# Weight sums in DRAM made in quarters of 512 KB with their copies on SP's queue, and retention's first operands loaded earlier

## The chip, the cores and the metric

The kernel runs on one core of a Trainium2 chip. The metric is the device time of one execution in microseconds (us). The core's engines are TensorE (PE in the profile, its weight loads PEld), VectorE (DVE), ScalarE (ACT), GpSimd (POOL) and SyncE (SP). Each runs its own instructions in order; semaphores tie them together. DMAs are issued by SP (queue q1 in the profile) and by GpSimd (queue q0).

## The reference, cut to what matters

One decoder block on x (1024 tokens, 1024 channels, float32). A normalised and modulated h goes through one wide projection, whose parts feed retention (4 heads, keys of 256, values of 512, in chunks of 128 tokens) and three groups of dilated attention:

```python
proj = h @ w_in
rq = rotary(heads(rq, 4), pos); rk = rotary(heads(rk, 4), pos) * 256 ** -0.5
ro = retention(rq, rk, heads(rv, 4))
ret_out = (silu(rg) * group_norm(ro)) @ w_ret_out
att_out = att @ w_att_out
merged = sigmoid(gate_a) * ret_out + sigmoid(gate_b) * att_out
x = x + g1 * (merged @ w_o)
x = x + g2 * (square(relu(h2 @ w1)) @ w2)
```

The change touches how the weights of rv (`w_rv`) and `w_ret_out` are prepared, and when retention's first q, k, v and gate weights are loaded.

## The kernel before

**Arithmetic.** Each float32 operand is split into a high part that TensorE takes as it is and a low rest: ScalarE copies the high part, VectorE subtracts it, and `mm3` (L201, L203, L205) makes three matmuls of 128x512 for one product. Large products are done by a scheme with seven block products in place of eight ("11", "s1", "s3", "s2", "12", "22", "s4" in `ORDER`), for which sums of weight blocks and sums of blocks of h are needed.

**The order of the work** is written out by hand: the program's order is each engine's order. The stages around the change are, in order, `av_first` and `av_step` (values of attention, PE `av`), `queries_keys` (PE `qap`), `values` (retention's values, PE `va`, `vb`, `vc`) and `chunk` (retention, PE `rg`, `kv`, `o`).

**Queries, keys and gates.** `queries_keys` runs 18 pairs of output blocks through the class `Blocks` (L243 to L285), seven products of 12 matmuls each, 84 matmuls a pair. For the pair two ahead, `before` issues two weight loads of 512 KB on SP (`a_load`, L874, tile `wa`) when a pair starts. `prep` splits a block of weights as soon as a slot is free (ScalarE L248, VectorE L258, tile `qaw`; sums of blocks on VectorE L243, tile `qas`), `post` evacuates the banks (L280, L284, L285, L903, L905), `rotate` (L927) applies the rotation to a pair of q or k, and results go to DRAM on SP (`aqd`, `gated` L915, `qkd` L930). Preparations and evacuations share ScalarE and VectorE in program order: a preparation that waits for a load or for a buffer holds up the evacuations behind it, and those give PE its banks back.

**The weight sums** are made in DRAM by DMAs that GpSimd issues (`weight_sums`, L541 to L551), called once at the start of `queries_keys`. Each of the two matrices has four blocks of 2 MB. `dma_sum` copies one operand (L535) and adds the other with an accumulating DMA (L536): s1 = b21 + b22, s3 = b21 + b11, s2 = s1 + b11, s4 = s2 + b12. Then three plain copies follow (L551). All are 2 MB, 22 DMAs in all (tiles `wrv..`, `wro..`). A small GpSimd multiply (L543) holds the first until the last sum of h is there.

**Retention's values.** `values` runs 14 products (i = 0 to 13), each in four quarters p of 12 matmuls. Weights of product i + 2 are loaded when product i starts (L984, `vwl`), and split during product i - 1 (`v_w`, `v_low`). Results that are complete are split (L1027 to L1034) into tiles `vo` of the pool `wraw`, or for "s4" into `vr`, and stored (L1036, `vd`). The pool `wraw` has three buffers, which the weight loads of `Steps` use as well.

**Retention's entry.** At the end of `values` come, before the change:

- at i = 12, p = 3: `fetch(0)`, which loads q and k of chunks 0 and 1 (L574, `qk`) and v of chunk 0 (L582);
- at i = 13, p = 0: eight restores of h from DRAM by GpSimd (L1061, L1062, `hh`, `hl`), and `first["release"]`, which lets `Steps` issue its next three loads (L85: gate weights and two rows of modulation weights);
- at i = 13, p = 1: `jit_qk(0)` and `jit_qk(1)`, which split q and k of chunks 0 and 1 (ScalarE L594, GpSimd L595, tile `j`);
- at i = 13, p = 2: `ahead(2)`, which splits the first gate weights (L191, L192) and takes one modulation product (L450).

Then the pool of the stage is closed, `fetch(1)` and `fetch(2)` follow, and `s_kt(0)` makes chunk 0's scores and transposed keys (PE `sT`, `kT`; L617 to L628, the last of them `kl`). The PSUM banks are laid out anew after it, and PE's first matmuls of retention (`rg`) wait for `kl`.

Of the kernel before, what the change touches and what calls it, by code (L numbers as in the profile page):

```python
# [11 lines left out]
F32 = mybir.dt.float32  # L12
F32R = mybir.dt.float32r
AF = mybir.ActivationFunctionType
ALU = mybir.AluOpType
AX = mybir.AxisListType

P = 128
D = 1024
S = 1024  # L20
NK = D // P
# [33 lines left out]
class Steps:  # L55
# [12 lines left out]
    def add(self, body, loads=(), manual=False):  # L68

        self.steps.append((list(loads), body, manual))  # L70
# [64 lines left out]
def block_kernel(ctx, tc, io, stop=None, dbg=None):  # L135
# [3 lines left out]
    def fv(t):  # L139
        return t.bitcast(F32)  # L140
# [385 lines left out]
    YB = ("11", "12", "21", "22")  # L526

    WN = ("11", "12", "22", "s1", "s2", "s3", "s4")
    wv_d = {n: dram.tile([P, 4, 1024], F32, name=f"wrv{n}") for n in WN}
    ws_d = {n: dram.tile([P, 4, 1024], F32, name=f"wro{n}") for n in WN}  # L530

    def dma_sum(out, x, y):

        flat = lambda t: t.rearrange("p a b -> p (a b)").rearrange("p (a b) -> p a b", b=2048)
        nc.gpsimd.dma_start(flat(out), flat(x))  # L535
        nc.gpsimd.dma_start(flat(out), flat(y), accum_op=ALU.add, max_dma_last_dim=8192)  # L536

    def weight_sums(t):

        for i, v in enumerate((VC_GNG, VC_GNB)):  # L540
            nc.vector.tensor_copy(gnv[i][:, :16], vec[:, v:v + 16])  # L541
            nc.vector.tensor_scalar_mul(gnv[i][:, 16:], vec[:, v:v + 16], -1.0)
        nc.gpsimd.tensor_tensor(pad[:, NK:NK + 1], fv(t)[:, :1], mhalf[:, :1], op=ALU.mult)  # L543
        for dst, src in ((wv_d, io["w_rv"]), (ws_d, io["w_ret_out"])):
            b11, b12, b21, b22 = (src[i] for i in range(4))
            dma_sum(dst["s1"], b21, b22)
            dma_sum(dst["s3"], b21, b11)
            dma_sum(dst["s2"], dst["s1"], b11)
            dma_sum(dst["s4"], dst["s2"], b12)
            for n, b in (("11", b11), ("12", b12), ("22", b22)):  # L550
                nc.gpsimd.dma_start(dst[n], b)  # L551

    def result_sums():
        b11, b12, b21, b22 = (y_d[:, i] for i in range(4))
# [10 lines left out]
    def fetch(i):  # L565

        h, c = divmod(i, NC)
        if i > 1:
            hd["qk", i] = R["p"].tile([P, 4, C], F32, tag="qk", bufs=4, name=f"qk{h}{c}")
        elif i == 0:  # L570
            t = whl.tile([P, 1024], F32, tag="wl", name="qk01").rearrange("p (a b c) -> p a b c", a=2, b=4)
            for j in range(2):
                hd["qk", j] = t[:, j]
                nc.sync.dma_start(t[:, j], qk_d[0][:, :, j * C:(j + 1) * C])  # L574
        if i > 1:
            nc.sync.dma_start(hd["qk", i], qk_d[h][:, :, c * C:(c + 1) * C])
        if i > 0:
            v = R["p"].tile([P, 2, DV], F32R, tag="V", bufs=4, name=f"v{h}{c}")
        else:
            v = whl.tile([P, 1024], F32R, tag="wh", name="v00").rearrange("p (a b) -> p a b", a=2)  # L580
        hd["v", i] = v
        nc.sync.dma_start(fv(v), v_d[h][:, c])  # L582
# [4 lines left out]
    def jit_qk(i):  # L587
        src = hd["qk", i]
        if i > 1:
            t = R["p"].tile([P, 2, 4, C], F32R, tag="j", bufs=2, name=f"j{i}")  # L590
        else:
            t = whl.tile([P, 1024], F32R, tag=("wh", "wl")[i], name=f"j{i}")
            t = t.rearrange("p (a b c) -> p a b c", a=2, b=4)
        nc.scalar.copy(t[:, 0], src)  # L594
        nc.gpsimd.tensor_sub(t[:, 1], src, fv(t[:, 0]))  # L595
        hd["j", i] = t
# [337 lines left out]

    def queries_keys(ahead):
        sums_of_h("t4")
        weight_sums(XA["t4", 3][1])
        sums = [(q, n) for q in range(NA) for n in ORDER][4:]
        while len(BA.slots) > 1:
            BA.prep(sums.pop(0))  # L940

        def before(q, n):
            if n == ORDER[0] and q + 2 < NA:
                for part in (1, 2):
                    a_load(q + 2, part)

        turns = []

        def after(q, n):
            if turns:  # L950
                next(turns[0], None) or None
            if n == ORDER[-1] and PAIRS[q][0] == "r":
                while turns:
                    drain(turns.pop())
                turns.append(rotate(q))
            if q == NA - 1 and n in ("12", "s4"):
                v_load(n == "s4")
            if q == NA - 1 and n == "22":
                for j in range(2):
                    v_w(0, j)  # L960

        BA.run([(q, n) for q in range(NA) for n in ORDER], sums, before, after)
        while turns:
            drain(turns.pop())
        values(ahead)


# [11 lines left out]
    def v_load(i):  # L979

        hp, n = VSEQ[i]
        for j in range(2):
            lo = V["w", i, j] = v_place(i, "l", j)
            nc.sync.dma_start(fv(lo), wv_d[n][:, 2 * hp + j])  # L984

    def v_w(i, j):
        lo, hi, sign = V["w", i, j], v_place(i, "h", j), float(VPLAN[VSEQ[i][1]][1])
# [4 lines left out]
    def v_low(i, j):  # L992
        lo, hi, sign = V.pop(("low", i, j))
        if sign > 0:
            nc.vector.tensor_sub(lo, fv(lo), fv(hi))
        else:
            nc.vector.scalar_tensor_tensor(lo, fv(lo), -1.0, fv(hi), op0=ALU.mult, op1=ALU.subtract)
# [12 lines left out]
    def v_post(i, p):  # L1010

        hp, n = VSEQ[i]
        ps = V["ps", VPLAN[n][2], p]
        if n == "11":
            V["r", p] = x4(f"vr{hp}{p}", F32R)
        r1, r2 = (fv(V["r", p])[:, 512 * j:512 * j + 512] for j in range(2))
        if n in ("11", "s2"):
            nc.scalar.copy(r1, ps)
            return
        if n == "s1":  # L1020
            nc.scalar.mul(r2, ps, -1.0)
            return
        t = V["r", p].rearrange("p (a b) -> p a b", a=2)
        if n != "s4":
            t = wraw.tile([P, 2, DV], F32R, tag="raw", name=f"vo{i}{p}")
        if n == "22":
            nc.scalar.mul(t[:, 0], ps, -1.0)  # L1027
            nc.vector.scalar_tensor_tensor(t[:, 1], ps, -1.0, fv(t[:, 0]), op0=ALU.mult, op1=ALU.subtract)
        else:

            src, dst = {"12": (r1, r1), "s3": (r2, r2), "s4": (r1, r2)}[n]
            (nc.vector.tensor_sub if n == "s3" else nc.vector.tensor_add)(dst, src, ps)
            nc.scalar.copy(t[:, 0], dst)
            nc.vector.tensor_sub(t[:, 1], dst, fv(t[:, 0]))  # L1034
        blk = {"12": "11", "s4": "12", "s3": "22", "22": "21"}[n]
        nc.sync.dma_start(v_d[2 * hp + int(blk[0]) - 1][:, p + 4 * (int(blk[1]) - 1)], fv(t))  # L1036

    def values(ahead):
        last = len(VSEQ) - 1
        for j in range(2):  # L1040
            v_low(0, j)
        for i, (hp, n) in enumerate(VSEQ):
            if i + 2 <= last:
                v_load(i + 2)
            for p in range(4):
                v_mm(i, p)
                if V["post"]:
                    v_post(*V["post"].pop())
                V["post"].append((i, p))
                if p < 2 and i < last:  # L1050
                    v_w(i + 1, p)
                    if p:
                        v_low(i + 1, 0)
                if p == 2 and i < last:
                    v_low(i + 1, 1)
                if i == last - 1 and p == 3:

                    fetch(0)
                if i == last and p == 0:
                    for m in range(4):  # L1060
                        nc.gpsimd.dma_start(hh[2 * m][:, 512:], h12_d[m][:, 0])  # L1061
                        nc.gpsimd.dma_start(hl[2 * m][:, 512:], h12_d[m][:, 1])  # L1062
                    first["release"]()
                if i == last and p == 1:
                    jit_qk(0)
                    jit_qk(1)
                if i == last and p == 2:
                    ahead(2)
        v_post(*V["post"].pop())
        open_ret()  # L1070
        for g in (1, 2):
            fetch(g)
        s_kt(0)
        banks(False)
# [559 lines left out]
    def r_w_load(i):  # L1634

        n, c = RSEQ[i]
        src = ws_d[n]
        for s in range(2):
            lo = r_place(i, "l", s)
            nc.sync.dma_start(fv(lo), src[:, 2 * c + s])  # L1640
            Q["w", i, s] = lo

    def r_place(i, part, s):
# [679 lines left out]
def _blocks(w):  # L2323

    t = _quads(w).reshape(2, 4, 2, P, 1024).transpose(1, 3, 0, 2, 4)
    return np.ascontiguousarray(t).reshape(4, P, 4, 1024)

def _vblocks(w):

    t = w.reshape(4, 2, P, 2, 2, 512).transpose(4, 1, 2, 3, 0, 5)  # L2330
    return np.ascontiguousarray(t).reshape(4, P, 4, 1024)

def _vcols(w, width):

# [94 lines left out]
```

## Time and profile before

| | |
|---|---|
| runs | 2280.99, 2286.97, 2281.17 us; median 2281.17 |
| profiled execution | 2277.95 us, span 2276.1 us, mean PE clock 0.99 |
| TensorE, VectorE, ScalarE, GpSimd busy | 96%, 64%, 40%, 6% of the span |
| DMA | 408.91 MB, mean 180 GB/s; SP's queue 43.4%, GpSimd's 10.2% of 16 engines |
| `qap` | from 159.5 to 530.5 us |
| `va`, `vb`, `vc` | from 530.6 to 685.4 us |
| retention's first matmul | 700.0 us |

In the profile's rows an instruction stands with its line, its engine, its output <- inputs by the program's names, and in brackets the idle time just before it and what ended it. In a list of waits the three numbers are us in total, times, and the longest. In the chain of work that ended last each row is start, length and what it was.

### The profile page before, as it was taken

How to read it: one execution, taken by the hardware profiler on the slowest of the kernel's cores; microseconds unless marked ns; L12 is line 12 of the kernel's file. 1: busy time of each engine (PE TensorE's matmuls, PEld its weight loads, DVE VectorE, ACT ScalarE, POOL GpSimd, SP SyncE). 2: the span in 40 equal slices, each digit the busy share in tenths (PEclk: the TensorE clock that was granted, in tenths of full speed). 3: DMA queues.
4: the chain of work that ended last, by engine and by line, in shares of the span. 5: the costliest groups of instructions: out<-in, count | busy, mean ns of one | idle time of the engine just before them, and what ended most of it. 6: DMA issues, size and time to landing. Idle time of an engine off the chain costs nothing.

```text
span 2276.1 us, 27081 instructions
## 1 busy us (share of the span) xinstructions
PE 2189.8 (96%) x10130; PEld 1808.0 (79%) x10130; DVE 1454.4 (64%) x2285; ACT 908.5 (40%) x1665; POOL 126.0 (6%) x143
## 2 busy tenths in 40 slices
PE   7999988999997999999999999999999999999998
PEld 5887867787885888888888888888777788788887
DVE  6527675773446788765554554576876665787845
ACT  4323222323333445444544533434454444433412
POOL 0000000000001121110000000001100000000003
PEclk9999999999998999999999999999999999999999
DMA  9539999226556465539831445645144443754322
GB/s 359 198 142 262 309 293 298 104 91 213 188 192 231 155 213 191 182 122 285 228 122 51 140 174 203 220 171 184 65 143 153 152 146 111 276 174 167 121 84 75
DMA packets 152866, 408.91 MB, mean 180 GB/s; under 512 B 26006, under 2 KB 53917, under 8 KB 148766
## 3 DMA queue, kind: packets, MB, share of 16 engines
q1 hardware_dynamic: 147262, 342.16, 43.4%
q0 software_dynamic: 5472, 65.01, 10.2%
q8 instruction: 80, 1.31, 0.2%
q14 instruction: 52, 0.43, 0.1%
HBM read 316.27 MB, written 156.13 MB: 208 GB/s over the span
## 4 chain that ended last, share of the span: by engine, by line
PE 75%; DVE 11%; DMA 5%; ACT 5%; issue 2%; SPq 0%; POOL 0%; POOLq 0%; DVEq 0%; ACTq 0%
PE av L742 4%; PE qap L201 3%; PE qap L205 3%; PE qap L203 3%; PE rg L201 3%; PE rg L203 3%; PE rg L205 3%; PE fp L201 2%; PE fp L203 2%; PE fp L205 2%; DMA wa<-in_w_rq_dram 2%; PE ak L201 2%; PE f2a L203 2%; PE f2a L205 2%; PE f2a L201 2%
## 5 line engine op out<-in xcount | busy, mean ns | idle before, releaser
L201 PE MATMUL qap<-hh,qaw 128*128 128x512 f32 x216 | 87.7, 406 | 19.9 <-DVE qat L285 10.7
L205 PE MATMUL qap<-hh,qaw 128*128 128x512 f32 x216 | 86.4, 400 | 0.0
L203 PE MATMUL qap<-hl,qaw 128*128 128x512 f32 x216 | 86.4, 400 | 0.0
L201 PEld LDWEIGHTS qap<-hh,qaw 128*128 128x128 f32 x216 | 42.0, 194 | 31.8 <-DVE qat L285 13.1
L1888 ACT ACTIVATE a<-a 128x512 f32<-128x512 f32 x48 | 30.3, 632 | 84.8 <-DVE a L1887 84.8
L1241 ACT ACTIVATE P<-P,ng 128x128 f32<-128x128 f32 (+1 forms) x96 | 41.9, 438 | 39.2 <-DVE ng L1238 39.2
L595 POOL TENSOR_TENSOR j<-qk,j 128x512 fp32r<-128x512 f32 x32 | 43.1, 1347 | 259.5 <-ACT j L594 259.5
L258 DVE TENSOR_TENSOR fw<-w1r,fw 128x512 fp32r<-128x512 f32 x48 | 32.9, 688 | 37.6 <-ACT fw L248 37.6
L258 DVE TENSOR_TENSOR qaw<-wa,qaw 128x512 fp32r<-128x512 f32 x54 | 37.0, 686 | 31.3 <-ACT qaw L248 31.3
L2072 ACT CAST w2h<-w2s 128x512 fp32r<-128x512 f32 x36 | 22.4, 621 | 77.9 <-DVE w2s L2110 74.9
L1785 POOL TENSOR_TENSOR accnf<-accnf,sqnf 128x256 f32<-128x256 f32 (+1 forms) x18 | 16.6, 922 | 624.1 <-ACT sqnf L1784 624.1
L201 PE MATMUL fp<-h2h,fw 128*128 128x512 f32 x128 | 50.0, 391 | 0.0
L617 ACT COPY sm<-sT 128x128 f32<-128x128 f32 x32 | 8.5, 266 | 103.7 <-PE sT L608 103.7
L203 PE MATMUL fp<-h2l,fw 128*128 128x512 f32 x128 | 49.8, 389 | 0.0
L201 PE MATMUL roa<-rh,rwl 128*128 128x512 f32 x128 | 49.8, 389 | 0.0
L203 PE MATMUL roa<-rl,rwh 128*128 128x512 f32 x128 | 49.8, 389 | 0.0
L205 PE MATMUL roa<-rh,rwh 128*128 128x512 f32 x128 | 49.8, 389 | 0.0
L205 PE MATMUL fp<-h2h,fw 128*128 128x512 f32 x128 | 49.8, 389 | 0.0
L248 ACT CAST qaw<-wa 128x512 fp32r<-128x512 f32 x54 | 32.4, 616 | 42.7 <-PE qap L205 16.3
L205 PEld LDWEIGHTS qap<-hh,qaw 128*128 128x128 f32 x216 | 42.0, 194 | 9.1
L203 PEld LDWEIGHTS qap<-hl,qaw 128*128 128x128 f32 x216 | 42.2, 195 | 8.7
L1622 DVE TENSOR_TENSOR rwl<-rwl,rwh 128x1024 fp32r<-128x1024 f32 x25 | 30.2, 1220 | 29.1 <-ACT rwh L1653 29.1
(3084 smaller groups left out, 7151.2 us busy)
## 6 DMA issues: line engine op xcount, KB each, us to landing
v<-vd SPq DMA_DIRECT2D x32, 512.0 KB, 4.9
raw<-in_w_ada_dram SPq DMA_DIRECT2D x32, 512.0 KB, 4.8
w1r<-in_w_ff_dram SPq DMA_DIRECT2D x32, 512.0 KB, 5.1
vd<-vo SPq DMA_DIRECT2D x24, 512.0 KB, 3.3
yt<-y POOLq DMA_DIRECT2D x6, 2048.0 KB, 15.3
xsd<-as SPq DMA_DIRECT2D x24, 512.0 KB, 2.7
w2r<-in_w_ff2s_dram SPq DMA_DIRECT2D x24, 512.0 KB, 7.8
em<-in_w_ada_dram SPq DMA_DIRECT2D x16, 512.0 KB, 10.2
```

Of the source, the lines that this page charges most:

```text
L201: nc.tensor.matmul(o, wl, xh, start=first, stop=False, skip_group_check=skip)
L203: nc.tensor.matmul(o, wh, xl, start=False, stop=False, skip_group_check=skip)
L205: nc.tensor.matmul(o, wh, xh, start=False, stop=last, skip_group_check=skip)
L248: nc.scalar.copy(t[:, :512], src)
L258: nc.vector.tensor_sub(t[:, 512:], src, fv(t[:, :512]))
L595: nc.gpsimd.tensor_sub(t[:, 1], src, fv(t[:, 0]))
L742: nc.tensor.matmul(av[g][c], x[k][:, c * C:(c + 1) * C], w[j][:, ws], start=k == 0 and (x, j) == parts[0], stop=k == NK - 1 and (x, j) == ...
L1241: nc.scalar.activation(v, v, AF.Exp, bias=ng[:, blk:blk + 1], accum_out=st[:, g, blk, 2 + a:3 + a])
L1622: nc.vector.tensor_sub(lo, fv(lo), fv(hi))
L1785: (nc.vector if f == 7 else nc.gpsimd).tensor_add(G["acc", key], G["acc", key], sq)
L1888: nc.scalar.activation(o, o, AF.Relu)
L2072: nc.scalar.copy(hi, src)
```

## The change

- **The sums are made by quarters.** `wv_d` and `ws_d` become, for each name, four tensors of 512 KB; the host packs the blocks so that a quarter is contiguous. For each quarter SP copies b21 into s1 (from block 2) and into s3, and b11, b12, b22 into their places: 40 copies. Behind the copy of s3, `quarter_sums` puts six DMAs on GpSimd's queue: add b22 to s1, add b11 to s3, copy s1 to s2, add b11, copy s2 to s4, add b12: 48 in all.
- **The copies are placed** one by one: four ahead of the first preparations, then one after the products "s1", "s2" and "12" of each pair until the list is empty (pair 11). The order of the list is s1 and s3 by quarters, then 11, 12, 22, first for `w_rv`, then for `w_ret_out`.
- The small GpSimd multiply goes; the signs of the group norm are set by `gn_signs` in the same place on VectorE.
- **Retention's operands move**: `fetch(0)` to i = 11, p = 2; `release` to i = 11, p = 3; `jit_qk(0)` and `jit_qk(1)` to i = 12, p = 1 and 2; `ahead(2)` to i = 12, p = 3. The restores of h stay at i = 13, p = 0. The tiles `vo` of products 11 and 12 come from the pool of the stage (`x4`) and no longer from `wraw`.

```diff
-    wv_d = {n: dram.tile([P, 4, 1024], F32, name=f"wrv{n}") for n in WN}
-    ws_d = {n: dram.tile([P, 4, 1024], F32, name=f"wro{n}") for n in WN}
+    wv_d = {n: [dram.tile([P, 1024], F32, name=f"wrv{n}{j}") for j in range(4)] for n in WN}
+    ws_d = {n: [dram.tile([P, 1024], F32, name=f"wro{n}{j}") for j in range(4)] for n in WN}
+    WB = {"s1": 2, "s3": 2, "11": 0, "12": 1, "22": 3}
+    copies = [(d, src, n, j) for d, src in ((wv_d, "w_rv"), (ws_d, "w_ret_out"))
+              for ns in (("s1", "s3"), ("11",), ("12",), ("22",)) for j in range(4) for n in ns]
+    def copy_block():
+        if copies:
+            d, src, n, j = copies.pop(0)
+            nc.sync.dma_start(d[n][j], io[src][WB[n], j])
+            if n == "s3":
+                quarter_sums(d, io[src], j)
+    def quarter_sums(d, src, j):
+        s1, s2, s3, s4 = (d[f"s{i}"][j] for i in (1, 2, 3, 4))
+        def add(out, x):
+            nc.gpsimd.dma_start(out, x, accum_op=ALU.add, max_dma_last_dim=8192)
+        add(s1, src[3, j])
+        add(s3, src[0, j])
+        nc.gpsimd.dma_start(s2, s1)
+        add(s2, src[0, j])
+        nc.gpsimd.dma_start(s4, s2)
+        add(s4, src[1, j])
...
-    def weight_sums(t):
+    def gn_signs():
...
-        nc.gpsimd.tensor_tensor(pad[:, NK:NK + 1], fv(t)[:, :1], mhalf[:, :1], op=ALU.mult)
-        for dst, src in ((wv_d, io["w_rv"]), (ws_d, io["w_ret_out"])):
-            b11, b12, b21, b22 = (src[i] for i in range(4))
-            dma_sum(dst["s1"], b21, b22)
-            dma_sum(dst["s3"], b21, b11)
-            dma_sum(dst["s2"], dst["s1"], b11)
-            dma_sum(dst["s4"], dst["s2"], b12)
-            for n, b in (("11", b11), ("12", b12), ("22", b22)):
-                nc.gpsimd.dma_start(dst[n], b)
...
     def queries_keys(ahead):
         sums_of_h("t4")
-        weight_sums(XA["t4", 3][1])
+        for _ in range(4):
+            copy_block()
+        gn_signs()
...
         def after(q, n):
+            if n in ("s1", "s2", "12"):
+                copy_block()
...
-            nc.sync.dma_start(fv(lo), wv_d[n][:, 2 * hp + j])
+            nc.sync.dma_start(fv(lo), wv_d[n][2 * hp + j])
...
-        if n != "s4":
+        if n != "s4" and i > len(VSEQ) - 4:
+            t = x4(f"vo{i}{p}", F32R).rearrange("p (a b) -> p a b", a=2)
+        elif n != "s4":
             t = wraw.tile([P, 2, DV], F32R, tag="raw", name=f"vo{i}{p}")
...
+                if i == last - 2 and p == 2:
+                    fetch(0)
+                if i == last - 2 and p == 3:
+                    first["release"]()
+                if i == last - 1 and p in (1, 2):
+                    jit_qk(p - 1)
                 if i == last - 1 and p == 3:
-                    fetch(0)
+                    ahead(2)
                 if i == last and p == 0:
                     for m in range(4):
                         nc.gpsimd.dma_start(hh[2 * m][:, 512:], h12_d[m][:, 0])
                         nc.gpsimd.dma_start(hl[2 * m][:, 512:], h12_d[m][:, 1])
-                    first["release"]()
-                if i == last and p == 1:
-                    jit_qk(0)
-                    jit_qk(1)
-                if i == last and p == 2:
-                    ahead(2)
...
-            nc.sync.dma_start(fv(lo), src[:, 2 * c + s])
+            nc.sync.dma_start(fv(lo), ws_d[n][2 * c + s])
```

The host's packing of the two matrices (`_blocks`, `_vblocks`) puts the quarter ahead of the partition. No other line of the kernel changes.

More of the change, by code (lines that the diff above doesn't have):

```diff
@@ L1636, in r_w_load @@
         n, c = RSEQ[i]
-        src = ws_d[n]
         for s in range(2):
             lo = r_place(i, "l", s)
-            nc.sync.dma_start(fv(lo), src[:, 2 * c + s])
+            nc.sync.dma_start(fv(lo), ws_d[n][2 * c + s])
             Q["w", i, s] = lo
@@ L2325, in _blocks @@
     t = _quads(w).reshape(2, 4, 2, P, 1024).transpose(1, 3, 0, 2, 4)
-    return np.ascontiguousarray(t).reshape(4, P, 4, 1024)
+    return np.ascontiguousarray(t.reshape(4, P, 4, 1024).transpose(0, 2, 1, 3))
 def _vblocks(w):
     t = w.reshape(4, 2, P, 2, 2, 512).transpose(4, 1, 2, 3, 0, 5)
-    return np.ascontiguousarray(t).reshape(4, P, 4, 1024)
+    return np.ascontiguousarray(t.reshape(4, P, 4, 1024).transpose(0, 2, 1, 3))
 def _vcols(w, width):
```

## The prediction

> **What bounds the kernel now.** I read the page's first lines, then the list of PE's waits, then the windows, the chain and the queues at the two stages that the diff touches.
>
> ```profile
> span 2276.1 us, 27081 instructions
> ...
> PE 2189.8 (96%) x10130; PEld 1808.0 (79%) x10130; DVE 1454.4 (64%) x2285; ACT 908.5 (40%) x1665; POOL 126.0 (6%) x143
> ```
>
> TensorE sets the end: it is busy for 2189.8 of 2276.1 us, so only what makes PE wait, or run at a lower clock, can be won. The diff changes no matmul. The list of waits says which idle time lies in reach:
>
> ```profile
> PE rg L201 <- DVE kl L628: 13.6, 1, 13.6
> PE qap L201 <- DVE qat L285: 10.7, 5, 5.9
> PE qap L201 <- ACT qat L280: 9.2, 2, 6.9
> ```
>
> The first is one wait at retention's entry, the other two are seven waits in the stage of queries, keys and gates (`qap`), while GpSimd sums weights in DRAM. Next, windows cut from the start of one pair of that stage (84 matmuls) to the start of the next:
>
> ```profile
> 159.52:183.22 23.70, 20.95 (x85) 16.39 (x84) 18.07 (x32) 11.18 (x20) 2.30 (x4) 0.93 0.84 257
> 278.42:308.51 30.09, 21.57 (x85) 17.04 (x84) 15.17 (x23) 5.12 (x9) 1.42 (x2) 0.89 0.93 287
> 308.51:328.38 19.87, 19.33 (x85) 15.69 (x84) 14.97 (x24) 6.75 (x12) 1.39 (x2) 1.00 1.09 343
> 328.38:347.42 19.04, 19.04 (x85) 15.77 (x84) 14.62 (x25) 6.53 (x12) 0.91 (x1) 1.00 0.89 223
> 366.46:393.21 26.75, 20.81 (x85) 16.76 (x84) 11.89 (x19) 3.49 (x6) 0.00 (x0) 0.87 1.00 329
> 393.21:416.31 23.10, 20.94 (x85) 16.82 (x84) 17.03 (x27) 8.63 (x15) 0.00 (x0) 0.93 0.34 129
> ```
>
> After the stretch and its length come PE, PEld, DVE, ACT, POOL, PE's clock, DMA share and GB/s. Pair 8 (328.38) shows the undisturbed price: 84 matmuls in 19.04 us, 0.2267 us each, 2.72 us for one product of 12. Against it pair 0 loses 4.66 us, pair 6 11.05, pair 7 0.83, pair 10 7.71 and pair 11 4.06. These losses hold idle time and the lower clock after it. The chain and ScalarE's rows tell what was late:
>
> ```profile
> 257.24 30.84 DMA wa<-in_w_gate_dram
> ...
> 294.39 15.37 DMA wa<-in_w_rq_dram
> ...
> 370.07 26.00 DMA wa<-in_w_rq_dram
> ```
> ```profile
> 288.10 0.62 ACT L248 CAST qaw<-wa 128x512 fp32r<-128x512 f32 x1 [12.71 <-DMA wa<-in_w_gate_dram]
> ...
> 309.78 0.62 ACT L248 CAST qaw<-wa 128x512 fp32r<-128x512 f32 x1 [3.76 <-DMA wa<-in_w_rq_dram]
> ...
> 383.45 0.62 ACT L248 CAST qaw<-wa 128x512 fp32r<-128x512 f32 x1 [8.76 <-DMA aqd<-qa]
> ```
>
> Pairs 6 and 7 waited for weight loads of 30.8 and 15.4 us; pairs 10 and 11 for a result store that kept a buffer (`aqd`), and for a load of 26 us. And this is what GpSimd's queue held at those times:
>
> ```profile
> 234.45 0.52 POOL L535 DMA_DIRECT2D wrvs<-wrvs  x1 [16.22 <-DMA wrvs<-in_w_rv_dram]
> 242.88 0.92 POOL L536 DMA_DIRECT2D wrvs<-in_w_rv_dram  x1 [7.92 <-DMA wrvs<-wrvs]
> 243.47 1.82 POOL L551 DMA_DIRECT2D wrv<-in_w_rv_dram  x3
> 244.94 0.83 POOL L535 DMA_DIRECT2D wros<-in_w_ret_out_dram  x1
> 287.00 0.91 POOL L536 DMA_DIRECT2D wros<-in_w_ret_out_dram  x1 [41.23 <-DMA wros<-in_w_ret_out_dram]
> ```
>
> At 242.88 to 244.94 five DMAs of 2 MB went out without a wait, and the queue took until 287 for these 10 MB; the load of 257.24 lies in just this stretch and landed at 288.08. Before that, with one or two of them queued, pairs 1 to 5 took 278.42 - 183.22 = 95.2 us, five times 19.04, and lost nothing. So it is the depth of that queue, not its mean traffic, that PE pays for. Pair 0's 4.66 us is something else: VectorE is busy for 18.07 of 23.70 us there with the last sum of h and the first preparations. The diff leaves that order as it is.
>
> **The change, part by part: the sums.** The same bytes are copied and added. Before, GpSimd issued 22 DMAs of 2 MB. After, SP issues the 40 first copies of 512 KB, four ahead of the stage and three in each pair up to pair 11, and GpSimd 48 DMAs of 512 KB, chained quarter by quarter: the two adds of a quarter go together, then copy, add, copy, add, each waiting for the one before. So at most about two or three of 512 KB stand in its queue, 1.5 MB in place of 10.
>
> ```profile
> q0 software_dynamic: 2848, 46.14, 62.6%
> q1 hardware_dynamic: 7308, 25.28, 26.1%
> ```
>
> These two rows (packets, MB, share of the 16 engines from 160 to 420 us) give packets of 16.2 KB for GpSimd's queue and 3.5 KB for SP's. The Trainium skill (DMA: Bandwidth & Descriptors, Queues, rings and completion order) says that a DMA engine takes turns between the queues that have work, a packet at a time; by that rule, which the load of 30.8 us agrees with, a load is held up by as many packets as wait in the other queue, and all of pairs 6 to 11's loss would go (2246.8).
>
> Does the summing still end in time? A 2 MB add took 16.2 us (the wait ahead of 234.45), a copy 7.9 (that ahead of 242.88). A quarter is then, estimated in proportion, 8.1 + 2 + 4.1 + 2 + 4.1 = 20.3 us, and 162 for eight; with 2 us more for each of the five steps 242, so until about 410. The first load of these weights comes in the last pair, which starts at 416.31 + 5 x 19.04 - 21.65 = 490. Nothing on GpSimd waits behind them but the next quarter; the wait for SP's copies that its adds gain costs nothing.
>
> The price is on SP's queue, where the copies stand among loads and stores. A copy of 512 KB is 2 us by the 7.9 above, 6 behind an add of its own size (4.1 + 2). The last copy of a pair is placed after its fifth product, two products (5.4 us) ahead of the next loads, so a load finds one ahead of it, seldom two. The slowest kind of load took, in the middle of eight,
>
> ```profile
> wa<-in_w_rq_dram SPq DMA_DIRECT2D x8, 512.0 KB, 16.1
> ```
>
> and I take 10 to 16 us for the new ones: 16 is the old row with an add of 2 MB in the other queue, 10 one with a quarter of that and one or two copies ahead. Their cover: the load of 257.24 was wanted at 288.10 - 12.71 = 275.39, 18.2 us after its issue; that of 294.39 at 306.02, 11.6 us after, and being 3.8 us late it cost pair 7 0.83 us. So a few such losses stay: two or three of 0.83, **2.0 us** (bounds: 0 and all 23.65). Gain of this part: 11.05 + 0.83 + 7.71 + 4.06 = 23.65, less 2.0: **21.65 us**. The first loads of pair 2 stand behind the four first copies, 8 us by the price above; a few us of ScalarE's waiting there find slack of some 6 us (12.71 of waiting made 6.9 of PE's), so 0.
>
> SP pays for 40 issues of 0.43 us (the middle number below, ns), 17 us in a queue that waits 135.7 us for one kind of result alone: 0.
>
> ```profile
> L874 SPq DMA_DIRECT2D wa<-in_w_rq_dram x6: 392/432/463, 204.5 to 370.6; - x6
> ```
> ```profile
> SPq L915 <- DVE qa L905: 135.7, 12, 32.1
> ```
>
> The weights' new layout changes only where the 512 KB loads `vwl` and `rwl` begin; they are issued two products of 4 x 2.72 us ahead, more than even 16.1: 0.
>
> **The change: retention's entry.** Rows of before:
>
> ```profile
> 677.27 0.69 DVE L1032 TENSOR_TENSOR vr<-vr,vc 128x512 f32<-128x512 f32 x1 [1.40 <-PE vc L205]
> ...
> 683.46 0.62 ACT L594 CAST j<-qk 128x512 fp32r<-128x512 f32 x1 [4.85 <-DMA qk<-qkd]
> ...
> 685.00 0.39 PE L205 MATMUL vc<-vwh,hh 128*128 128x512 f32 x1
> ...
> 690.62 1.04 ACT L191 CAST raw_4649h<-raw 128x1024 fp32r<-128x1024 f32 x1 [2.60 <-DMA raw<-in_w_rg_dram]
> ...
> 696.15 0.68 DVE L1032 TENSOR_TENSOR vr<-vr,vc 128x512 f32<-128x512 f32 x1
> ...
> 699.47 0.48 DVE L628 SCALAR_TENSOR_TENSOR kl<-kT,ct,kh 128x256 fp32r<-128x256 f32 x1
> ...
> 700.01 1.22 PE L201 MATMUL rg<-hh,raw_4649l 128*128 128x512 f32 x2 [13.59 <-DVE kl L628]
> ```
>
> The last product of values ends at 685.4. ScalarE stood twice for `qk` and once for the gate weights, in order, so the last result of values (L1032) came only at 696.15, and `kl`, behind which PE stood, at 699.95. After, the three fetches and the release of the gate weights are issued five quarter products earlier (13.6 us), `j0` four (10.9), `j1` and the gate weight's split three (8.2). On SP the fetches and the release each pass five stores of products 11 and 12; on GpSimd `j0` and `j1` pass the eight restores of h. The stretch that takes them:
>
> ```profile
> 650.00:660.00 10.00, 10.00 (x46) 8.29 (x45) 3.12 (x5) 4.34 (x6) 0.00 (x0) 1.00 0.13 52
> 660.00:670.00 10.00, 10.00 (x46) 8.29 (x45) 6.43 (x9) 4.35 (x6) 0.00 (x0) 1.00 0.53 210
> ```
>
> The DMA engines are busy for 0.53 at most there, ScalarE has 5.6 us of 10 for the 2.3 us that it gains (683.46, its twin and 690.62) and VectorE 3.6 for the split and one product of the modulation (two passes over 128x1024, an estimated 2 to 3 us by ScalarE's 1.04). The results of products 11 and 12 get other buffers, so the loads needn't wait for those stores. Two further loads of the next gate weights wait for VectorE's split, and the last stores of values stand behind them on SP; only `sm` waits for one of these stores, 8 us later. So none of the old waits is left, and what is late next is the rest of the chain itself: L1032 of the last quarter follows PE as the first did, at 677.27 + 3 x 2.72 = 685.43, and from L1032 to PE's start it takes 700.01 - 696.15 = 3.86 us. PE starts at 689.3 in place of 700.0: **10.7 us**.
>
> Next in line are the restores of h, since the second halves of `j0` and `j1` on GpSimd now stand before them:
>
> ```profile
> L595 POOL TENSOR_TENSOR j<-qk,j 128x512 fp32r<-128x512 f32 x32 | 43.1, 1347 | 259.5 <-ACT j L594 259.5
> ```
> ```profile
> 678.08 0.53 POOL L1062 DMA_DIRECT2D hl<-h12d  x1 [1.14 <-issue]
> ```
> ```profile
> hl<-h12d POOLq DMA_DIRECT2D x4, 256.0 KB, 7.9
> ```
>
> The last lands at about 678.6 + 7.9 = 686.5, after (2 x 1.35 us more) at 689.2 at the latest, and the first matmuls need the first pair only. So 0, with 4 us as the far end. The clock:
>
> ```profile
> 700.00:710.00 10.00, 9.98 (x39) 7.92 (x39) 2.00 (x3) 0.27 (x1) 0.00 (x0) 0.83 0.73 238
> ```
>
> 39 matmuls in place of 44 cost about 1.1 us after the wait of 13.6; pair 0, with much shorter waits, shows 0.93 of the clock too, so I take 0 and keep 1.1 as a bound.
>
> **Sum.** The profiled execution took 2277.95 us (1.85 around the span). 2277.95 - 21.65 - 10.7 = 2245.6. The median of the runs, 2281.17, is 3.2 above it, so I forecast 2248.8.
>
> **Rivals.** *The sums go no lighter.* The same bytes cross the same engines in the same 12 pairs at a DMA share of 0.89 (62.6 + 26.1%) already, and only the entry is won: 2281.17 - 10.7 = 2270.5. For it speaks the share, against it that pairs 1 to 5 ran beside the same traffic and lost nothing. The Trainium skill (same page, Issuing engines are not separate DMA queues) speaks for it: whoever issues, the transfers interleave on the same engines. I give 0.12.
>
> *Copies in front of loads: slower.* SP's queue is served in order, and a store or load now stands behind copies that also share the engines with adds. If three copies came ahead at 6 us each, a load would take 16 + 18 = 34 us, more than that of 257.24, and each such pair would lose pair 6's 11.05. The gain of 34.35 is gone from 3.1 such pairs on; with pairs 0 to 5, where the first quarters lie thickest, it is 2281.17 - 34.35 + 66.3 = 2313. Against it: the copies are placed at different products, at least 5 us apart. 0.11.
>
> *The entry comes forward only partly*, because the restores or the second keys' load end last: 4 to 8 us of the 10.7 are lost, about 2255. 0.10.
>
> **How the numbers follow.** Forecast 0.67, with its own range 2242 (all of 23.65, 10.7 and 1.1 won, and some 3 us of scatter between runs) to 2256. The range goes on to 2264, about half of pairs 6 to 11's loss kept, and leaves out 0.18: the first two rivals but for a part of the first. A measurement of this kernel tells about 0.3%, 6.8 us, from no change. Faster by more: 0.67 + 0.10 + 0.09 of the first rival = 0.86. Within: 0.03 + 0.02 = 0.05. Slower: 0.09.
>
> **What would show it.** In the new profile: pairs 6, 7, 10 and 11 at 19 to 20 us and pair 0 still near 23.7; no weight load in the chain above some 16 us; the wait of `rg` for `kl` near 3 us with no wait of ScalarE for `qk` or the gate weights. I am wrong if PE's waits in `qap` move to other pairs, if ScalarE waits for loads behind copies, or if `rg` waits for `hh`.

## The result, and the profile after

The kernel after takes **2246.86 us** (median of 4 runs, 2244.46 to 2248.68) against 2281.08 for the kernel before beside it: a ratio of **0.9844, 95% interval 0.9825 to 0.9862**. The forecast was 2248.8. A second set of runs gave 2246.15 and 0.9855 [0.9835, 0.9876].

The profiled execution took 2244.46 us. Its page begins:

```profile
span 2242.7 us, 27133 instructions
...
PE 2182.0 (97%) x10130; PEld 1804.8 (80%) x10130; DVE 1454.8 (65%) x2285; ACT 908.4 (41%) x1665; POOL 145.4 (6%) x168
```

The span is 33.4 us shorter. PE is busy for 7.8 us less with the same 10130 matmuls: in the four pairs that waited its clock was 0.87 to 1.00, now it is 1.00 in all of them (the windows below). The other 25.6 us were idle time. The same windows as before, each from the start of a pair to the start of the next (pairs 0, 6, 7, 10, 11; columns: stretch, length, PE, PEld, DVE, ACT, POOL, PE's clock, DMA share, GB/s):

```profile
159.38:182.41 23.03, 19.65 (x86) 15.62 (x84) 18.07 (x32) 11.14 (x20) 2.30 (x3) 1.00 0.99 314
277.61:296.65 19.04, 19.04 (x86) 15.77 (x84) 14.82 (x24) 5.74 (x10) 1.29 (x2) 1.00 0.87 282
296.65:315.69 19.04, 19.04 (x86) 15.77 (x84) 13.81 (x22) 5.91 (x11) 2.89 (x4) 1.00 0.98 276
353.77:372.81 19.04, 19.04 (x86) 15.77 (x84) 15.04 (x25) 5.64 (x10) 3.68 (x5) 1.00 0.94 296
372.81:391.85 19.04, 19.04 (x86) 15.77 (x84) 13.89 (x22) 6.17 (x11) 1.30 (x2) 1.00 0.94 284
```

From pair 1 on every pair takes 19.04 us: the four that lost 23.65 us lose nothing, at a DMA share of 0.87 to 0.98 (0.93, 1.09, 1.00 and 0.34 in the longer windows of before). Pair 0 loses 3.99 in place of 4.66. The queues from 160 to 420 us (packets, MB, share of 16 engines):

```profile
q1 hardware_dynamic: 9223, 49.05, 48.9%
q0 software_dynamic: 2960, 24.12, 43.5%
```

SP's queue now carries most of the bytes; the sum of the shares, 92%, is a little above the old 89%. The traffic didn't get lighter. What got shorter is the longest load of weights in the stage. These are the answers for the tile `wa`, 160 to 480 us, from issue to landing, first before, then after. (The trace tells the landing of only some of the 32 loads of the stage, 16 before and 14 after; the medians and maxima here and below are of those.)

```profile
DMA to landing us min/median/max: 4.3/10.2/30.8
```
```profile
DMA to landing us min/median/max: 4.3/7.1/13.0
```

And retention's entry, whose lines moved: L1032 is now L1054, L594 is L610, L617 is L633, L628 is L644.

```profile
660.55 0.39 PE L205 MATMUL vc<-vwh,hh 128*128 128x512 f32 x1
...
660.97 0.69 DVE L1054 TENSOR_TENSOR vr<-vr,vc 128x512 f32<-128x512 f32 x1 [0.66 <-PE vc L205]
...
664.10 0.27 ACT L633 COPY sm<-sT 128x128 f32<-128x128 f32 x1 [1.78 <-DMA vd<-vr]
...
665.75 0.48 DVE L644 SCALAR_TENSOR_TENSOR kl<-kT,ct,kh 128x256 fp32r<-128x256 f32 x1
...
666.28 1.22 PE L201 MATMUL rg<-hh,raw_4661l 128*128 128x512 f32 x2 [4.71 <-DVE kl L644]
```

From the end of the last product of values to `rg` it was 700.01 - 685.39 = 14.62 us; it is 666.28 - 660.94 = 5.34. ScalarE waits neither for `qk` nor for the gate weights. In the trace of the second set the same stretch is 6.33. Pairs (28.31 - 3.99 = 24.3) and entry (9.3) make 33.6 us; from `rg` to the end it is 1576.4 us in place of 1576.1. What is left in the entry is the row at 664.10: `sm` waits for a store of `vr`.

### The profile page after: what moved, and what is told of

It reads as the page before. It is cut to its first block, busy times and chain, and to the rows that moved or that the text cites. A ratio compares the mean times of both kernels' runs of the same rounds, so it can differ in the third digit from the quotient of the medians.

```text
span 2242.7 us, 27133 instructions
## 1 busy us (share of the span) xinstructions
PE 2182.0 (97%) x10130; PEld 1804.8 (80%) x10130; DVE 1454.8 (65%) x2285; ACT 908.4 (41%) x1665; POOL 145.4 (6%) x168
## 4 chain that ended last, share of the span: by engine, by line
PE 44%; DVE 8%; ACT 4%; issue 2%; DMA 1%; POOL 0%; SPq 0%; POOLq 0%; DVEq 0%; ACTq 0%
PE fp L201 2%; PE fp L203 2%; PE fp L205 2%; PE f2a L203 2%; PE f2a L201 2%; PE f2a L205 2%; PE ak L201 2%; PE ak L203 2%; PE ak L205 2%; PE wo L201 1%; PE wo L203 1%; PE wo L205 1%; PE roa L205 1%; PE roa L203 1%; PE roa L201 1%
## 5 line engine op out<-in xcount | busy, mean ns | idle before, releaser
L201 PE MATMUL qap<-hh,qaw 128*128 128x512 f32 x216 | 84.3, 390 | 3.4 <-DVE qat L285 1.7
L205 PE MATMUL qap<-hh,qaw 128*128 128x512 f32 x216 | 84.1, 389 | 0.0
L1909 ACT ACTIVATE a<-a 128x512 f32<-128x512 f32 x48 | 30.3, 632 | 84.9 <-DVE a L1908 84.9
L633 ACT COPY sm<-sT 128x128 f32<-128x128 f32 x32 | 8.5, 266 | 102.2 <-PE sT L624 100.4
L1806 POOL TENSOR_TENSOR accn<-accn,sqn 128x512 f32<-128x512 f32 x12 | 15.5, 1294 | 477.9 <-ACT sqn L1805 477.9
## 6 DMA issues: line engine op xcount, KB each, us to landing
em<-in_w_ada_dram SPq DMA_DIRECT2D x16, 512.0 KB, 10.2
```

Source lines behind the costliest of these rows:

```text
L201: nc.tensor.matmul(o, wl, xh, start=first, stop=False, skip_group_check=skip)
L205: nc.tensor.matmul(o, wh, xh, start=False, stop=last, skip_group_check=skip)
L633: nc.scalar.copy(sm, ps[:, :C])
L1806: (nc.vector if f == 7 else nc.gpsimd).tensor_add(G["acc", key], G["acc", key], sq)
L1909: nc.scalar.activation(o, o, AF.Relu)
```

## The experiments

Theory: the two parts act separately; the first wins by the **depth** of GpSimd's queue, and what the entry lacks is the wait of `sm`. Rivals: the size of the DMAs or the queue they stand on decides; the slower mechanism (copies ahead of loads) is near.

### Each part alone

```diff
 e1_sums_only: the kernel after, with
-    fetch(0), release, jit_qk, ahead(2) at i = 11 and 12; vo of products 11, 12 in x4
+    fetch(0) at i = 12, p = 3; release, jit_qk, ahead(2) at i = 13; vo in wraw
 e2_entry_only: the kernel before, with just those lines of the kernel after
```

> The kernel after with its entry put back as it was before: the sums by quarters alone. If the two parts are independent, the stage of queries and keys keeps what it gained (its pairs lose 4.0 us in place of 28.3) and the wait of rg stays at 13.6: 2281.1 - 24.3 = 2256.8 us. If one part needs the other (the whole gain of 34.2 is not the sum), the time lies over 2260 or the entry is shorter than 14.6 us from the start of the last matmul of values.

> The kernel before with retention's operands loaded earlier, the sums as before. If the entry's gain is its own, 9.3 us go: 2271.8 us, and sm waits for the store of vr as in the kernel after (wait of rg 4.7 us). Rival, the entry is faster only because the sums end earlier or in other DMAs: 2276 or more, and rg waits longer than 4.7 us.

The sums alone took 2254.71 us, ratio 0.9862 [0.9836, 0.9889]; the entry alone 2275.33, 0.9965 [0.9947, 0.9982]. Their product, 0.9827, lies within the interval of both together. In the trace of the first, pairs lose 4.2 us in all and the entry takes 13.7, 0.9 less than the 14.6 that I had set as the sign of independence; in that of the second, pairs lose 31.8 and the entry takes 6.3, with the same wait of `sm` (2.8 us). There `rg` waits 5.7 us, not 4.7, but so it does in the second trace of the kernel after: the entry of the same code differs by 1 us between executions. Within that, the parts are independent. The second gained 8 us, not 9.3. The four pairs of a kernel with a deep queue vary from run to run (28.3 and 31.8 us lost), which is why the entry's 8 us show only over many runs.

### The old DMAs with a shallow queue

```diff
 e3_depth_one: the kernel before, with
+    def landed(t):
+        nc.gpsimd.dma_start(seen_d, t[:, 0, :16])
...
     dma_sum(dst["s1"], b21, b22)
+    landed(dst["s1"])
...
     for n, b in (("11", b11), ("12", b12), ("22", b22)):
         nc.gpsimd.dma_start(dst[n], b)
+        landed(dst[n])
```

(The same behind s3 and s4. The tiny DMA has to wait for the landing of what it reads, and with it GpSimd.)

> The kernel before with its sums of 2 MB on GpSimd, as large and as many, but behind each DMA that was unchained a tiny DMA reads a few columns of what it wrote, so that GpSimd waits and about two of 2 MB stand in its queue, not five. Theory (the depth of the queue is what pairs 6, 7, 10 and 11 paid for): these four lose 3 us or less in all and the time is about 2281.1 - 21 = 2260. Rival (what helps is smaller DMAs, or the copies on SP's queue): they still lose 15 to 24 us and the time is 2275 to 2285.

It took **2255.89 us, 0.9875 [0.985, 0.9899]**: as fast as the quarters alone. GpSimd's rows of two of the copies that stood five deep before:

```profile
271.18 0.50 POOL L559 DMA_DIRECT2D wrv<-in_w_rv_dram  x1
281.07 0.53 POOL L541 DMA_DIRECT2D seen<-wrv  x1 [9.38 <-DMA wrv<-in_w_rv_dram]
281.59 0.50 POOL L559 DMA_DIRECT2D wrv<-in_w_rv_dram  x1
292.74 0.54 POOL L541 DMA_DIRECT2D seen<-wrv  x1 [10.65 <-DMA wrv<-in_w_rv_dram]
```

and pairs 6 and 10, with the loads of the whole stage:

```profile
278.12:297.16 19.04, 19.04 (x86) 15.77 (x84) 14.83 (x24) 5.74 (x10) 2.05 (x4) 1.00 0.84 305
...
354.28:373.32 19.04, 19.04 (x86) 15.77 (x85) 15.04 (x25) 5.64 (x10) 1.98 (x3) 1.00 0.82 268
```
```profile
DMA to landing us min/median/max: 4.4/11.3/14.6
```

Same 2 MB DMAs, same queue, same bytes, and no loss. The median load is even slower than before (11.3 against 10.2); only the slowest went, 30.8 to 14.6. From 160 to 420 us GpSimd's queue has 60.2% of the engines against 62.6% before; from 166 to 394, while the old sums ran, 61.4% against 71.3%. More than in this mean, the two differ while a load is on its way. These are the queues (packets, MB, share) of before from 261 to 283.5 us, in which the load of 30.8 us waited, and then of this run from 277.5 to 285, between two of its copies:

```profile
q0 software_dynamic: 160, 7.34, 92.6%
q1 hardware_dynamic: 160, 0.59, 7.6%
```
```profile
q1 hardware_dynamic: 404, 1.52, 61.3%
...
q0 software_dynamic: 48, 0.01, 0.8%
```

As long as both queues have work, they send packet for packet, 160 and 160; but those of GpSimd's copies are large (46 KB on average against 3.7), so SP's queue moves 0.59 MB in 22.5 us, little more than one load. When GpSimd has to wait, its queue runs empty between two DMAs, and the loads catch up.

Neither small DMAs nor SP's queue are needed for the gain of the first part; a dozen tiny DMAs that make GpSimd wait do it.

### Small DMAs with a deep queue

```diff
 e6_copies_on_gpsimd: the kernel after, with
-            nc.sync.dma_start(d[n][j], io[src][WB[n], j])
+            nc.gpsimd.dma_start(d[n][j], io[src][WB[n], j])
 e9_gpsimd_held: e6, and at the start of queries_keys
+        nc.gpsimd.tensor_tensor(pad[:, NK:NK + 1], fv(XA["t4", 3][1])[:, :1], mhalf[:, :1], op=ALU.mult)
```

> The kernel after with its 40 copies issued by GpSimd in place of SP, at the same places of the program. Each matrix's twelve copies of 11, 12 and 22 follow one another without a wait, 6 MB of small DMAs in GpSimd's queue at once, with the next quarter's behind them. Theory (depth): the loads that fall in these two stretches take 18 to 25 us, PE loses about 5 us in each, 2247 + 10 = 2257. Rival (the size of the DMAs decides): no load over 16 us and 2245 to 2249.

2285.88 us, 1.0011 [0.9994, 1.0027]: the whole gain is gone, more than either theory expected. Two rows of GpSimd, and two lists of waits, ScalarE's and PE's, up to 216 us:

```profile
19.66 1.22 POOL L541 DMA_DIRECT2D wrvs<-in_w_rv_dram  x2
...
169.58 3.67 POOL L541 DMA_DIRECT2D wrv<-in_w_rv_dram  x7
```
```profile
ACT avo L764 <- DMA vad<-avo: 17.2, 1, 17.2
```
```profile
PE qap L201 <- DVE qaw0s L258: 14.9, 1, 14.9
```

This run also changed something that I had not meant: on GpSimd nothing holds the copies, so the sums began at 19.66 us, in the middle of the stages before (`qap` starts at 176.3 in place of 159.4, 16.9 us late), and the first twelve unchained copies fell into the end of attention's values, where a store of 256 KB kept ScalarE for 17.2 us and pair 0 lost 20.0. Hence the second one, with the multiply that held the sums in the kernel before:

> The kernel with all 40 copies on GpSimd, and the small GpSimd multiply put back ahead of them, so that none starts before the last sum of h, as in the kernel before. Theory (what cost 37 us was that GpSimd, which waits for nothing there, ran the copies ahead of their place into the stages of attention's values; eight of 512 KB in the queue, 4 MB, are within the loads' slack): no pair loses over 2 us but pair 0, 2247 to 2251. Rival (copies on GpSimd's queue are dear as such): it stays over 2265.

2260.10 us, 0.9892 [0.9873, 0.9911]. Most of the loss was the early start, but not all: my expectation missed by 9 us. Pairs lose 12.8 us, of which 8.45 in pair 8, behind the twelve copies and the next two (GpSimd's rows; then pair 8; then the loads of the stage):

```profile
293.68 3.68 POOL L541 DMA_DIRECT2D wrv<-in_w_rv_dram  x7
299.73 0.49 POOL L541 DMA_DIRECT2D wrv<-in_w_rv_dram  x1 [2.37 <-DMA wrvs<-in_w_rv_dram]
...
310.67 0.49 POOL L541 DMA_DIRECT2D wros<-in_w_ret_out_dram  x1 [1.29 <-DMA wrv<-in_w_rv_dram]
323.94 0.81 POOL L549 DMA_DIRECT2D wros<-in_w_ret_out_dram  x1 [12.78 <-DMA wros<-in_w_ret_out_dram]
```
```profile
316.28:343.77 27.49, 22.87 (x85) 17.76 (x84) 17.10 (x27) 7.23 (x13) 2.90 (x4) 0.88 0.93 255
```
```profile
DMA to landing us min/median/max: 4.5/7.6/20.8
```

GpSimd issues a further copy whenever one lands, so some eight stand from 294 to 311 and the queue isn't empty until 324: 7 MB, in DMAs of 512 KB. The first load of that stretch takes 20.8 us, and ScalarE waits 3.2 us for it; VectorE waits 6.3 us, until 324.8, for the one behind it, issued at 295.6, whose 29 us the answer above doesn't hold. Pair 8 pays 8.45. Smaller DMAs without a wait between them are a deep queue as well. (Some 5 us of this run's distance to the kernel after lie behind `rg`, in stages that the edit doesn't touch; they stay unexplained.)

### A backlog by itself

```diff
 e8_backlog: the kernel after, with, at the start of pair 13
+                for b in range(5):
+                    nc.gpsimd.dma_start(flat2(idle_d[b]), flat2(io["w_rv"][b % 4]))
 e11_backlog_three: the same with range(3)
```

> The kernel after with five plain copies of 2 MB more, issued by GpSimd without a wait behind its last sum (about 424 us, pair 13), into tensors that nobody reads. Theory (10 MB standing in GpSimd's queue hold SP's loads and stores up, whatever they are): loads and stores issued just after take about 30 us, the pairs after it lose 8 to 12 us, 2257. Rival (the adds and their chain make the loss, not the backlog): no load over 16 us, under 1 us lost, 2247 to 2248.

> The kernel with the plain copies that nobody reads behind the last sum, three of 2 MB in place of five. Theory (a load takes as long as the queue needs for what stands in it, 2.9 us a MB by 10 MB in 29 us, and has some 18 us of slack): loads issued behind these 6 MB take some 16 to 18 us and pair 15 loses 0 to 2 us, 2247 to 2249. Rival (a loss in proportion to the backlog): three fifths of 12.8, 7.7 us, 2254.

The five took 2260.12 us (0.9917 [0.9897, 0.9937], 14.0 above the kernel after beside it), the three 2250.93 (0.9862 [0.9841, 0.9883]). Of the five: GpSimd's row, what ScalarE waited for, pair 15, and the loads from 428 to 470 us.

```profile
421.52 2.74 POOL L968 DMA_DIRECT2D idle<-in_w_rv_dram  x5
```
```profile
452.74 0.62 ACT L248 CAST qaw15s<-qas 128x512 fp32r<-128x512 f32 x1 [15.52 <-DMA aqd<-qa]
459.40 0.60 ACT L924 ACTIVATE qa<-qap 128x512 f32<-128x512 f32 x1 [6.05 <-DMA aqd<-qa]
```
```profile
448.86:480.69 31.83, 22.84 (x85) 17.96 (x84) 17.04 (x27) 8.72 (x15) 0.00 (x0) 0.84 0.50 189
```
```profile
DMA to landing us min/median/max: 10.5/19.9/29.2
```

Plain copies, no add, no chain, and the picture of pairs 6 and 10 is there again: a load of 29.2 us, stores that keep `qa` and a slot, and 31.83 - 19.04 = 12.79 us, of which 8.99 idle and 3.80 slower matmuls at a clock of 0.84. With three:

```profile
445.58 0.62 ACT L248 CAST qaw15s<-qas 128x512 fp32r<-128x512 f32 x1 [7.45 <-DMA aqd<-qa]
```
```profile
449.78:468.82 19.04, 19.04 (x85) 15.77 (x84) 14.42 (x23) 6.52 (x12) 0.00 (x0) 1.00 0.21 77
```
```profile
DMA to landing us min/median/max: 5.1/10.3/15.4
```

ScalarE waits 7.45 us in place of 15.52, and PE loses nothing in this execution. In both runs the slowest load lands only when the backlog has gone: 3.0 us after the last of the five copies, 4.2 after the last of the three. So the load's time follows the backlog (29.2 and 15.4 us), while PE pays only for what goes beyond the slack of loads and stores: its price isn't in proportion. The profiled execution was the fastest of four (2246.4); the median, 2250.93, is 2 us above the range that I expected, and the others, up to 2254.2, have no trace: whether they lost those few us in pair 15 is not shown.

### Copies right ahead of the loads

```diff
 e5_copies_ahead_of_loads: the kernel after, with
             if n == ORDER[0] and q + 2 < NA:
+                for _ in range(3):
+                    copy_block()
                 for part in (1, 2):
                     a_load(q + 2, part)
...
-            if n in ("s1", "s2", "12"):
-                copy_block()
```

> The kernel after, but the three copies of a pair stand on SP's queue right ahead of the pair's two loads of weights, not spread over the pair. The slower rival of the prediction (three copies ahead at 6 us each) makes loads of 34 us, 11 us lost in each of some ten pairs, 2350 us. Theory: copies of 512 KB without adds in front cost 2 us each, with adds beside them up to 4, so loads take 15 to 20 us, within the 18 us and the slack that they have: 0 to 1 us a pair, 2247 to 2257.

2253.15 us, 0.9889 [0.9869, 0.9909]. The loads of the stage, and ScalarE's two longest waits for them:

```profile
DMA to landing us min/median/max: 4.2/10.4/18.9
```
```profile
183.46 0.62 ACT L248 CAST qaw<-wa 128x512 fp32r<-128x512 f32 x1 [3.75 <-DMA wa<-in_w_rk_dram]
...
394.44 0.62 ACT L248 CAST qaw<-wa 128x512 fp32r<-128x512 f32 x1 [3.39 <-DMA wa<-in_w_aq_dram]
```

Even with three copies in front, the slowest load takes 18.9 us, not 34 (of 12 loads whose landing is told; ScalarE's waits are told for all, and the longest is 3.75); pairs 1, 3 and 12 lose 1.03, 1.25 and 0.60. That is 2.9 of the 7.8 us by which its span is longer than that of the kernel after; 4.5 are in the entry, where `sm` waited 6.25 us for its store. Why longer than in the kernel after, with the same code there, is open.

### The rest of the entry

```diff
 e7_split_later: the kernel after, with
-                if i == last - 1 and p == 3:
+                if i == last and p == 2:
                     ahead(2)
 e10_sm_elsewhere: the kernel after, with, ahead of s_kt(0)
+        R["p"].tile([P, 1024], F32, name="gap0")
```

> The kernel after, but the first gate weights are split (and the two loads behind that split issued) three quarters of a product later, at i = 13, p = 2. Theory: sm waited for the store of vr because that store shares the DMA engines with those two loads; now the store lands in some 7 us, sm doesn't wait, the wait of rg is 3.0 to 3.5 us in place of 4.7, and the time is 1.4 us lower, about 2245.5. Rival: the eight restores of h hold the store up, sm still waits 1.5 us or more and rg 4.7, or the later split takes the place of that wait: 2247 or more.

> The kernel after, run again beside the next ones on the same chip: 2247 us, ratio 0.984.

> The kernel after with 4 KB left free in the pool of retention ahead of sm, so that sm no longer lies over the tile vr that the last store but three still reads; loads, stores and splits stay in their places. Theory (this store alone is what the entry lacked): ScalarE copies sm right behind its last result of values, rg's wait falls from 4.7 or 5.7 to 2.7 to 3.3, and the time is 1.5 to 2.5 us below that of the kernel after, about 2244.5. Rival: kl, which now lies over another tile, or the restores of hh keep rg waiting, 4.7 or more, 2246 to 2247.

The later split took 2245.44 us (0.9851 [0.9833, 0.9869]) beside 2246.15 for the kernel after: no difference that these runs can tell. Its trace shows both theories at work (ScalarE; then PE):

```profile
659.41 1.04 ACT L191 CAST raw_4661h<-raw 128x1024 fp32r<-128x1024 f32 x1
...
665.66 0.62 ACT L1055 CAST vr<-vr 128x512 fp32r<-128x512 f32 x1 [1.36 <-DVE vr L1054]
666.18 0.26 ACT L633 COPY sm<-sT 128x128 f32<-128x128 f32 x1
```
```profile
668.80 1.22 PE L201 MATMUL rg<-hh,raw_4661l 128*128 128x512 f32 x2 [4.59 <-DVE kl L644]
```

`sm` no longer waits, but the split now stands among the last results of values and makes them late: a wait for a wait, 4.59 us for `rg` where I had expected 3.0 to 3.5. With `sm` in another place of the pool, 2245.10 us (0.983 [0.9814, 0.9846]):

```profile
663.17 0.69 DVE L1054 TENSOR_TENSOR vr<-vr,vc 128x512 f32<-128x512 f32 x1 [0.65 <-PE vc L205]
```
```profile
663.89 0.62 ACT L1055 CAST vr<-vr 128x512 fp32r<-128x512 f32 x1 [2.10 <-DVE vr L1054]
664.42 0.26 ACT L633 COPY sm<-sT 128x128 f32<-128x128 f32 x1
```
```profile
667.04 1.22 PE L201 MATMUL rg<-hh,raw_4661l 128*128 128x512 f32 x2 [3.26 <-DVE kl L644]
```

ScalarE copies `sm` right behind its last result, and from L1054 to `rg` it is 667.04 - 663.17 = 3.87 us, the 3.86 that the prediction took from the trace of before; the entry takes 3.91 us, 10.7 less than before. So that store was all that was missing. In time it is 1 to 2 us (2246.86 and 2246.15 for the kernel after, though not in the same set): the lowest median of all, by hardly more than the runs scatter.

## Why the prediction was right

**The four pairs: the cause was right, the residual 2.0 us was mis-sized.** All of 23.65 us went, and 0.67 more in pair 0, which the prediction left alone; every other trace in which the sums start in their place shows 3.8 to 4.6 there, the one with the old deep queue 4.07, so the 4.66 was that one execution's. The step "it is the depth of that queue, not its mean traffic" is shown from both sides: the depth alone taken away won all of it (2255.89), and a backlog alone put in brought it back (12.79 us in one pair). The residual was made from loads of 10 to 16 us; they took 7.1 in the middle and 13.0 at most, where the rows gave 18.2 and 11.6 us as their cover. (Those are the 14 loads whose landing is told, and the ones that made pairs 6 and 7 late before are not among them; but neither ScalarE nor VectorE waits for any load of the stage.) The only wait of ScalarE for a DMA that is left in the stage with over 2 us is one of 2.1.

**The copies on SP** were priced too low: 2 to 6 us each, where the medians are 7.3 to 15.1 from issue to landing. It did no harm: the loads behind them were not held for as long, with one ahead 13.0 us at most, with three 18.9. So the slower rival's 18 us for three copies never came; two more copies cost the slowest load 6 us.

**The end of the sums** was put at about 410 us; GpSimd's last issue is at 423.9, 32 us a quarter in place of 30.3. The first use is in the last pair, from 487 us, so nothing waited.

**The entry: 9.3 us, not 10.7; the step that failed is "only `sm` waits for one of these stores, 8 us later".** The store was issued at 654.91 and `sm`, ready by 662.3, got its place at 664.1: it took 9 us, among eight restores of h, a load of gate weights and one of modulation weights. The prediction named this wait and let it go at a distance of 8 us, with stores at 7 to 8 us in its own rows (the restores 7.9). The chain behind it (3.86) was right, as the run with `sm` elsewhere shows. PE did not wait for the restores of h, as said. The clock was put at 0 as well: over the 10 us from `rg` it is 0.76 (37 matmuls) in place of 0.83 (39), no gain but a small loss, and from `rg` to the end it is 0.3 us longer.

**The total.** 34.2 us by medians against 32.4 forecast. The two mis-sized terms have opposite signs: 2.0 (and 0.67 in pair 0) more than the sum had, 1.4 less in the entry. That the forecast is within 2 us of the median is in part this luck.

**The rivals.** *The sums go no lighter* was right in its premise, the share of the DMA engines is as high as before (92%), and wrong in what follows from it. The Trainium skill (DMA: Bandwidth & Descriptors, Queues, rings and completion order) says that a DMA engine takes turns between queues packet by packet. The trace agrees: from 261 to 283.5 us, while the load of 30.8 us waited, the two queues sent 160 packets each. But the prediction drew the wrong conclusion from it, that a load is held up by as many packets as wait in the other queue. By turns it is held up by one of them for each packet of its own and of what stands ahead of it in SP's queue, and here each of those was a large one. So the depth counts because a deep queue of such copies doesn't run empty while the load is on its way: with 2 MB at a time it did, and the slowest load went from 30.8 to 14.6 us. *The entry only partly* came true in small: 1.4 of 10.7 us.

## What to carry to other kernels

Before trimming traffic, look at how many bytes one engine issues without a wait beside the loads that TensorE needs: compare the longest load, not the median, with the time between its issue and its use. A wait between large background transfers can be worth as much as making them small; and a queue whose engine waits for nothing runs ahead of its place in the program. When loads are moved forward, follow each store that a new tile must wait for, and where the wait can't be shortened, put the tile elsewhere.

## What the runs showed of the hardware

- Two DMA queues with work sent packet for packet, 160 and 160 in 22.5 us of before, whatever their size: 7.34 MB of DRAM copies and sums against 0.59 MB of loads and stores.
- So a load behind a backlog of large copies lands when the backlog has gone: behind 10 MB (five plain copies) a load of 512 KB took 29.2 us, behind 6 MB 15.4; PE lost 12.8 and 0 us in these two traces.
- DMAs of 512 KB, refilled as they land, hold loads as well: 20.8 and, by VectorE's wait, 29 us beside 7 MB in some 30 us.
- A wait can cost more than its length: 8.99 us idle in pair 15 went with 3.80 us more for the same matmuls (clock 0.84 over the pair). The clock needn't be lower after a longer wait: over the 10 us from `rg` it is 0.83 after 13.6 us of waiting (before), 0.76 after 4.7 (after) and 0.84 after 3.3 (`sm` elsewhere).
